# Products and sums of the modulation tables moved from VectorE to GpSimd, dealt out evenly from the third pair of feed-forward columns

## The chip, the cores and the metric

The kernel runs on one core of a Trainium2 chip. The metric is the device time of one execution in microseconds. Engines are named as in the profile: PE is TensorE, DVE VectorE, ACT ScalarE, POOL GpSimd, and SP the queue that issues the loads.

## The reference, cut to what matters

Two layers act on 256 rows of `x` and 256 rows of a context, 1024 wide. Each layer is a feed-forward, a mixer (gated linear attention, a short convolution, latent attention) and a second feed-forward. All are steered by modulation tables, nine parts of 1024 columns for each layer, made from one vector for `x` and one for the context:

```
for l in range(DEPTH):
    mod_x = jnp.split((sc @ ada_w[l] + ada_b[l])[:, None, :], N_MOD, axis=-1)
    mod_c = jnp.split((scc @ ada_w[l] + ada_b[l])[None, None, :], N_MOD, axis=-1)
    x = _ffn_step(x, mod_x, 0, ffn_w13[l, 0], ffn_w2[l, 0], ln_w[l, 0], ln_b[l, 0])
    ctx = _ffn_step(ctx, mod_c, 0, ffn_w13[l, 0], ffn_w2[l, 0], ln_w[l, 0], ln_b[l, 0])
    ...
```

`ada_w[l]` is 1024 x 9216 in fp32. `sc` and `scc` are single rows, so the two products read 38 MB a layer for two rows of output. In the last layer the context needs no parts 5 to 8.

## The kernel before, in words

**Weights.** Every large matrix is multiplied in three passes: a weight tile of 128 x 1024 fp32 is loaded by SP into one of five `raw` buffers (`NRAW`), ACT rounds it to `wh` (line 187), DVE takes the rest `wl = raw - wh` (line 188), and PE does wh by high, wh by low and wl by high (lines 232 to 235). There are three `wh` and three `wl` buffers (`NSPL`), and splits are made two tiles ahead (`AHEAD`). The order of all loads is that of the calls of `g.w`, recorded in a dry run of the program (`plan`); a load is issued as soon as one of the five buffers is free. Weight tiles and tiles of `ada_w` share this row and these buffers.

**Steps.** A feed-forward's first product (`ffn_in`) goes by 11 pairs of columns, p = 0 to 10, of 4 weight tiles each (two for `a`, two for `g`). One weight tile is one step: 24 matmuls with 512 columns. After a pair come SiLU, product and split (lines 730 to 735). Work left over from the stage before is called between steps: `pend` (transposes of the last rows) and `late` (renewing and storing the residual, lines 590 to 594).

**Modulation tables.** The first two parts of layer 0 are made on PE (`ada_group`). All others are made by the generator `ada_part` (lines 426 to 452): a part is eight tiles of `ada_w` of 128 x 1024; for each, DVE adds the tile times one column of `csil` to `acc`, for each stream (`x`, context) and each half of 512 columns. That is four DVE instructions a tile with two streams, two with one. Then PE sums `acc` over partitions with a matrix of ones (`pick`, line 448), DVE adds the bias to a `modrow` (line 384), and either POOL stores it to DRAM (line 387, parts 2, 5 and 8) or PE transposes it into `modT`. The bias tile `adab` is cleared by POOL (line 402) and loaded by SP (line 404).

A part has 12 units (`yield`) with two streams, 8 with one: one for each tile (two tiles with one stream), the rest for the end. `feeds` holds the parts under way. `feed(n)` runs n units; `feed_share(steps)` runs the units left over the steps left, rounded up. Units are dealt out at four places, which are called here by letters:

- **A**, the first feed-forward of layer 0: parts 2, 3, 4, two streams.
- **B**, the end of the mixer of layer 0: parts 5, 6, 7, two streams, one unit a step through `side`.
- **C**, the second feed-forward of layer 0: part 8, then parts 0 and 1 of layer 1, two streams.
- **D**, the first feed-forward of layer 1: parts 2, 3, 4 with two streams, 5 to 8 with one.

Each stage ends with `feed(10 ** 6)`: all its parts are done before the next begins.

**Buffers.** `T` is a pool of 9 tiles of 128 x 512, `U` one of 50. Before, `acc` lies in `T`, with `adab`, `modrow`, the `sil` tiles and the residuals `res`.

**POOL before** clears tiles, takes reciprocal roots for the norms (lines 581, 740 and 741) and issues some stores.

Of the kernel before, what the change touches and what calls it, by code (L numbers as in the profile page):

```python
# [13 lines left out]
ALU = mybir.AluOpType  # L14
# [8 lines left out]
NFB = DFF // P  # L23
# [275 lines left out]
def build(ctx, tc, aps, out, plan=None):  # L299

    g = Core(ctx, tc, aps, plan)
    nc = tc.nc
    act, dve, pe, pool, sp = nc.scalar, nc.vector, nc.tensor, nc.gpsimd, nc.sync
# [67 lines left out]
    csil = g.const([P, 8, 32], "csil")  # L371
# [8 lines left out]
    def ada_end(l, starts, ps, bias, streams):  # L380

        nq = 256
        row = g.T(name="modrow")
        dve.tensor_tensor(row[:, :nq], ps[:, :nq], bias[:, :nq], op=ALU.add)
        for q, c0 in enumerate(starts):
            if (c0 // D) % 3 == 2:
                pool.dma_start(modD[l][:streams, c0:c0 + nq], row[32 * q:32 * q + streams, :nq])
        yield
        if any((c0 // D) % 3 < 2 for c0 in starts):
            nj = nq // P  # L390
            pst = g.PS("adaT")
            for j in range(nj):
                transpose(pst[:, j * P:(j + 1) * P], row[:, j * P:(j + 1) * P])
            p4 = pst[:, :nj * P].rearrange("p (j q r) -> p q j r", j=nj, q=4)
            for q in (0, 2):
                k = starts[q] // P
                dve.tensor_copy(modT[l][:, k:k + 2 * nj, :].rearrange("p (q j) s -> p q j s", q=2), p4[:, q:q + 2, :, 0:2])
        yield

    def ada_bias(l, starts):  # L400
        bias = g.T(name="adab")
        pool.memset(bias[:, :256], 0.0)
        for q, c0 in enumerate(starts):
            sp.dma_start(bias[32 * q:32 * q + 2, :256], A_["ada_b"][l, c0:c0 + 256].partition_broadcast(2))
        return bias
# [20 lines left out]
    def ada_part(l, part, streams):  # L426


        starts = [part * D + 256 * q for q in range(4)]
        bias = ada_bias(l, starts)  # L430
        acc = [[g.T(name="acc") for _ in range(2)] for _ in range(streams)]
        for k in range(8):
            w = g.w([(R["ada_w"][l][k * P:(k + 1) * P, part * D:(part + 1) * D], D)], 1, split=False)
            for s_ in range(streams):
                for half in range(2):
                    a, b = acc[s_][half], w[:, 0, half * 512:(half + 1) * 512]
                    if k == 0:
                        dve.tensor_scalar(a, b, scalar1=csil[:, k, s_:s_ + 1], scalar2=None, op0=ALU.mult)
                    else:
                        dve.scalar_tensor_tensor(a, b, csil[:, k, s_:s_ + 1], a, op0=ALU.mult, op1=ALU.add)  # L440
            del w
            if streams == 2 or k % 2:
                yield
        yield
        ps = g.PS("ada")
        for s_ in range(streams):
            for q in range(4):
                pe.matmul(ps[32 * q:32 * q + 32, :256], pick[:, 1 - s_:33 - s_], acc[s_][q // 2][:, (q % 2) * 256:(q % 2 + 1) * 256],
                          start=s_ == 0, stop=s_ == streams - 1)
        del acc  # L450
        yield
        yield from ada_end(l, starts, ps, bias, streams)

    feeds = []

    def feed_parts(l, parts, streams=2):
        for part in parts:
            feeds.append([ada_part(l, part, streams), (8 if streams == 2 else 4) + 4])

    def feed(n):  # L460
        while n > 0 and feeds:
            try:
                next(feeds[0][0])
                feeds[0][1] -= 1
                n -= 1
            except StopIteration:
                feeds.pop(0)

    def feed_share(steps):

        left = sum(n for _, n in feeds)
        feed(-(-left // max(steps, 1)))

    def mod_ab(l, i, ln):

# [230 lines left out]
    def ffn_in(l, j, hT, tiles, gT, pend, late, opening=None):  # L706
        parts = parts_of(tiles)
        full = slice(0, parts[-1].stop)
        w13 = R["ffn_w13"][l, j]
        tiles_of = lambda c0, ps: g.fm_tiles(w13, c0, 8, g.pair_outs(ps), parts)  # L710
        psa, psg = {}, {}
        for p in range(NFB // 2):
            if p == 0 and opening is not None:
                psa[0], psg[0], psa[1] = [[g.PS("a") for _ in range(2)] for _ in range(3)]
                opening(tiles_of(0, psa[0]), tiles_of(DFF, psg[0]), tiles_of(256, psa[1]))
            else:
                tl = []
                if p not in psa:
                    psa[p] = [g.PS("a") for _ in range(2)]
                    tl += tiles_of(p * 256, psa[p])  # L720
                psg[p] = [g.PS("g") for _ in range(2)]
                tl += tiles_of(DFF + p * 256, psg[p])
                for n, _ in enumerate(g.fm(tl, hT, parts, group=3 if p == 0 and len(parts) > 1 else 1)):
                    if pend and n >= 1:
                        pend.pop(0)()
                    if late and p >= 1:
                        late.pop(0)()
                    feed_share(4 * (NFB // 2 - p) - 2 - n)
            for b in range(2):
                s = g.T(name="sil")  # L730
                act.activation(s[:, full], psa[p][b][:, full], AF.Silu)
                dve.tensor_tensor(s[:, full], s[:, full], psg[p][b][:, full], op=ALU.mult)  # L732
                h, lo = g.pairs(1, "g")[0]
                g.split(h[:, full], lo[:, full], s[:, full])
                gT.append((h, lo))
        feed(10 ** 6)
# [593 lines left out]
    for t in range(4):  # L1330
        a = A_["x"][0] if t < 2 else A_["ctx"][0]
# [23 lines left out]
    def opening(ta, tg, tb):  # L1355

        mm = lambda t, w, part, bs=(0, 1): g.mm3([(
            t[2][b][2][:, part], (w[0][:, kk, b * P:(b + 1) * P], w[1][:, kk, b * P:(b + 1) * P]),
            (hT[k][0][:, part], hT[k][1][:, part]), k == 0 and part.start == 0, k == 7 and part.stop == 512)
            for b in bs for kk, k in enumerate(t[1])], 0)  # L1360
        full = slice(0, 512)
        second = half_table(1)
        mod_ab0(0)
        bring((0, 1), 0)
        g.hold(2)
        wa, wg = g.w(ta[0][0], 4), g.w(tg[0][0], 4)
        for n, (t, w, part) in enumerate(((ta, wa, X), (tg, wg, X), (ta, wa, C), (tg, wg, C))):
            mm(t[0], w, part)
            if n == 0:
                bring((2, 3), 0)  # L1370
            if n == 1:
                g.early(1)
            next(second)
            next(second)
        del wa, wg, w
        next(second)
        g.early(1)
        wb = g.w(tb[0][0], 4)
        mm(tb[0], wb, full, (0,))
        run_all(second)  # L1380
        mod_ab0(1)
        bring((0, 1), 1)
        mm(tb[0], wb, full, (1,))
        g.hold(2)
        for t in (2, 3):
            load_x(t, 1)
        wa, wg = g.w(ta[1][0], 4), g.w(tg[1][0], 4)
        mm(ta[1], wa, X)
        bring((2, 3), 1)
        g.hold(None)  # L1390
        mm(tg[1], wg, X)
        mm(ta[1], wa, C)
        mm(tg[1], wg, C)
        wb = g.w(tb[1][0], 4)
        mm(tb[1], wb, full)
        feed_parts(0, (2, 3, 4))

    pend, late = [load_small] + [lambda: None] * 3 + [small_vectors], []
# [5 lines left out]
    for l in range(DEPTH):  # L1404
        last = l == DEPTH - 1
        tiles = [0, 1, 2, 3]
        if last:
            feed_parts(l, (2, 3, 4))
            feed_parts(l, (5, 6, 7, 8), 1)
        gT = []  # L1410
        ffn_in(l, 0, hT, tiles, gT, pend, late, opening if l == 0 else None)
        k1 = kept(f"h{l}a")
        pend, late = project_ln(gT, NFB, R["ffn_w2"][l, 0], tiles, l, 0, 0.5, ln_inputs(tiles, l, 0, res), k1, mod_ab(l, 1, (l, 0)),
# [10 lines left out]
        if not last:  # L1424
            feed_parts(l, (8,))
            feed_parts(l + 1, (0, 1))
        gT = []
        ffn_in(l, 1, hT, tiles, gT, pend, late)
        if last:
            o2 = out[0]  # L1430
# [15 lines left out]
def emit(tc, aps, out):  # L1446
    plan = build(None, Null(), {n: Null() for n in aps}, Null())
    with ExitStack() as ctx, tc.manual_schedule():
        build(ctx, tc, aps, out, plan)
# [18 lines left out]
```

## Time and profile before

| what | us |
|---|---|
| median of 3 runs (2699.78 to 2702.04) | 2700.31 |
| the profiled execution's own time | 2701.05 |
| its span in the profile | 2699.2 |
| PE busy in the span | 2621.2 |
| DVE busy | 1602.1 |
| ACT busy | 982.3 |
| POOL busy | 81.3 |

The sum of the prediction is made against the profiled execution, 2701.05 us; the median of the runs is 0.7 us lower. Busy times of the engines overlap. PE's mean granted clock over the span is 0.987 of full speed.

### The profile page before, as it was taken

What the parts mean: (1) busy time and instruction counts of PE and PEld (TensorE: products, weight loads), DVE (VectorE), ACT (ScalarE), POOL (GpSimd) and SP (SyncE); (2) the same over time, 40 slices, a digit from 0 to 9 for tenths busy, and PEclk for the clock granted to TensorE, in tenths of its full rate; (3) what the DMA queues carried; (4) which work ended last, traced back from release to release, by engine and by line L of the source; (5) the groups of instructions that cost most, each with busy time, mean ns of one, the idle gap of its engine ahead of it and who ended that gap; (6) DMA issues with size and microseconds to landing.
All of it is one profiled execution on the core that took longest, in us unless ns stands there. A gap on an engine that the chain in (4) does not pass through costs nothing. (4 is left out here: it accounts for less than half of the span.)

```text
span 2699.2 us, 36225 instructions
## 1 busy us (share of the span) xinstructions
PE 2621.2 (97%) x14243; PEld 2234.0 (83%) x14243; DVE 1602.1 (59%) x2429; ACT 982.3 (36%) x1565; POOL 81.3 (3%) x149
## 2 busy tenths in 40 slices
PE   8999999999999999999999979899999999999998
PEld 6888888888887888877888867788888988998996
DVE  3656256765453677468653389654367745567655
ACT  2222234545433232333222131223145653444442
POOL 0000000000000000000000000000010000100000
PEclk9999999999999999999999999899999999999999
DMA  7545353223221745546542456655443343567555
GB/s 251 175 152 164 114 166 98 67 63 120 78 75 59 226 150 155 165 134 194 169 137 98 157 159 206 213 175 168 154 133 102 108 130 100 174 179 227 180 188 171
DMA packets 324609, 400.63 MB, mean 148 GB/s; under 512 B 28403, under 2 KB 241935, under 8 KB 324439
## 3 DMA queue, kind: packets, MB, share of 16 engines
q1 hardware_dynamic: 321623, 391.99, 46.2%
q0 software_dynamic: 2816, 6.34, 0.6%
q8 instruction: 111, 1.82, 0.3%
q14 instruction: 59, 0.48, 0.1%
HBM read 382.49 MB, written 15.77 MB: 148 GB/s over the span
## 5 line engine op out<-in xcount | busy, mean ns | idle before, releaser
L188 DVE TENSOR_TENSOR wl<-raw,wh 128x1024 fp32r<-128x1024 f32 (+1 forms) x529 | 639.3, 1214 | 581.8 <-ACT wh L187 304.4
L187 ACT ACTIVATE wh<-raw 128x1024 fp32r<-128x1024 f32 (+1 forms) x529 | 549.0, 1050 | 794.2 <-PE tm L233 310.7
L232 PE MATMUL a<-hTh,wh 128*128 128x512 f32 (+1 forms) x784 | 271.0, 359 | 22.1 <-ACT wh L187 13.0
L440 DVE SCALAR_TENSOR_TENSOR acc<-raw,csil,acc 128x512 f32<-128x512 f32 x392 | 267.7, 749 | 0.0
L233 PE MATMUL a<-hTl,wh 128*128 128x512 f32 (+1 forms) x752 | 260.7, 359 | 1.3 <-DVE hTl L531 1.0
L232 PE MATMUL g<-hTh,wh 128*128 128x512 f32 (+1 forms) x704 | 247.3, 362 | 3.9 <-ACT wh L187 3.9
L233 PE MATMUL g<-hTl,wh 128*128 128x512 f32 (+1 forms) x688 | 241.2, 361 | 0.0
L232 PE MATMUL tm<-wh,gh 128*128 128x512 f32 x616 | 240.3, 390 | 0.0
L233 PE MATMUL tm<-wh,gl 128*128 128x512 f32 x616 | 239.7, 389 | 0.0
L232 PEld LDWEIGHTS a<-hTh,wh 128*128 128x128 f32 x784 | 153.2, 195 | 48.8 <-ACT wh L187 14.2
L233 PEld LDWEIGHTS a<-hTl,wh 128*128 128x128 f32 x752 | 146.9, 195 | 21.7 <-DVE hTl L531 2.6
L235 PE MATMUL tm<-wl,gh 128*128 128x512 f32 x616 | 163.4, 390 | 0.6 <-DVE wl L188 0.6
L235 PE MATMUL a<-hTh,wl 128*128 128x512 f32 (+1 forms) x752 | 157.9, 352 | 0.8 <-DVE wl L188 0.8
L232 PEld LDWEIGHTS g<-hTh,wh 128*128 128x128 f32 x704 | 134.0, 190 | 26.6 <-ACT wh L187 4.5
L240 ACT ACTIVATE gh<-sil 128x512 fp32r<-128x512 f32 (+1 forms) x88 | 50.9, 578 | 279.3 <-DVE sil L732 279.3
L235 PE MATMUL g<-hTh,wl 128*128 128x512 f32 (+1 forms) x688 | 149.4, 359 | 0.0
L233 PEld LDWEIGHTS g<-hTl,wh 128*128 128x128 f32 x688 | 130.6, 190 | 19.2
L235 PEld LDWEIGHTS a<-hTh,wl 128*128 128x128 f32 x752 | 125.9, 191 | 19.8 <-DVE wl L188 1.0
L235 PEld LDWEIGHTS tm<-wl,gh 128*128 128x128 f32 x616 | 115.4, 188 | 25.7 <-DVE wl L188 1.9
L233 PEld LDWEIGHTS tm<-wh,gl 128*128 128x128 f32 x616 | 115.7, 188 | 23.8
L232 PEld LDWEIGHTS tm<-wh,gh 128*128 128x128 f32 x616 | 115.6, 188 | 23.8
L235 PEld LDWEIGHTS g<-hTh,wl 128*128 128x128 f32 x688 | 117.9, 189 | 19.4
(323 smaller groups left out, 4705.0 us busy)
## 6 DMA issues: line engine op xcount, KB each, us to landing
raw<-in_ffn_w_dram SPq DMA_DIRECT2D x279, 512.0 KB
raw<-in_w_in_dram SPq DMA_DIRECT2D x156, 512.0 KB
raw<-in_ada_w_dram SPq DMA_DIRECT2D x128, 512.0 KB
raw<-in_w_out_dram SPq DMA_DIRECT2D x20, 512.0 KB
raw<-in_ada_w_dram SPq DMA_DIRECT2D x32, 256.0 KB
raw<-in_mla_proj_dram SPq DMA_DIRECT2D x16, 512.0 KB
raw<-in_gla_proj_dram SPq DMA_DIRECT2D x16, 512.0 KB
raw<-in_conv_proj_dram SPq DMA_DIRECT2D x16, 512.0 KB
```

The lines of the kernel that those rows point to most:

```text
L187: nc.scalar.activation(hi[:, :n], raw[:, :n], AF.Copy)
L188: nc.vector.tensor_tensor(lo[:, :n], raw[:, :n], hi[:, :n].bitcast(F32), op=ALU.subtract)
L232: mm(out, lhs[0], rhs[0], start=start, stop=False)
L233: mm(out, lhs[late], rhs[1 - late], start=False, stop=False)
L235: mm(out, lhs[1 - late], rhs[late], start=False, stop=stop)
L240: nc.scalar.activation(hi, src, AF.Copy)
L440: dve.scalar_tensor_tensor(a, b, csil[:, k, s_:s_ + 1], a, op0=ALU.mult, op1=ALU.add)
```

## The change

DVE's `acc = raw * csil + acc` becomes two POOL instructions, a product into a new `T` tile `prod` and a sum; a part's first tile needs the product alone. `acc` moves from `T` to `U`. `feed_share` keeps a running fraction in place of rounding up, it is called from p = 2 on and only where no `late` job is called, and it aims at an end within the last pair. The unit counts come out as before (12 and 8).

```diff
-        acc = [[g.T(name="acc") for _ in range(2)] for _ in range(streams)]
+        acc = [[g.U(name="acc") for _ in range(2)] for _ in range(streams)]
...
-                    if k == 0:
-                        dve.tensor_scalar(a, b, scalar1=csil[:, k, s_:s_ + 1], scalar2=None, op0=ALU.mult)
-                    else:
-                        dve.scalar_tensor_tensor(a, b, csil[:, k, s_:s_ + 1], a, op0=ALU.mult, op1=ALU.add)
+                    to = a if k == 0 else g.T(name="prod")
+                    pool.tensor_scalar(to, b, scalar1=csil[:, k, s_:s_ + 1], scalar2=None, op0=ALU.mult)
+                    if k:
+                        pool.tensor_tensor(a, a, to, op=ALU.add)
...
-            feeds.append([ada_part(l, part, streams), (8 if streams == 2 else 4) + 4])
+            feeds.append([ada_part(l, part, streams), 8 * streams // 2 + 4])
...
+    owed = [0.0]
+
     def feed_share(steps):
 
-        left = sum(n for _, n in feeds)
-        feed(-(-left // max(steps, 1)))
+        owed[0] += sum(n for _, n in feeds) / max(steps, 1)
+        n = int(owed[0])
+        owed[0] -= n
+        feed(n)
...
                     if late and p >= 1:
                         late.pop(0)()
-                    feed_share(4 * (NFB // 2 - p) - 2 - n)
+                    elif p >= 2:
+                        feed_share(4 * (NFB // 2 - 1 - p) + 2 - n)
```

How the instructions stand, at three places.

SP in stage D, before: the loads behind the first weight tiles (`in_ffn_w_dram`) of the stage; `in_ada_w_dram` are tiles of the modulation tables.

```order
L176 DMA raw_12304<-in_ffn_w_dram 128x4x256
L176 DMA raw_12352<-in_ffn_w_dram 128x4x256
L176 DMA raw_12360<-in_ffn_w_dram 128x4x256
L176 DMA raw_12380<-in_ada_w_dram 128x1024
L176 DMA raw_12432<-in_ada_w_dram 128x1024
L176 DMA raw_12464<-in_ada_w_dram 128x1024
L176 DMA raw_12512<-in_ada_w_dram 128x1024
L176 DMA raw_12526<-in_ada_w_dram 128x1024
L404 DMA adab_12552<-in_ada_b_dram 2x256 x4
L176 DMA raw_12566<-in_ada_w_dram 128x1024
```

With the change, SP in stage D from the 12th weight tile on (`h0c` is the stored residual, a `late` job):

```order
L176 DMA raw_13288<-in_ffn_w_dram 128x4x256
L598 DMA h0c<-r_12568 128x512
L176 DMA raw_13321<-in_ffn_w_dram 128x4x256
L598 DMA h0c<-r_12822 128x512
L176 DMA raw_13354<-in_ada_w_dram 128x1024
L598 DMA h0c<-r_12603 128x512
L176 DMA raw_13387<-in_ada_w_dram 128x1024
L598 DMA h0c<-r_12843 128x512
L176 DMA raw_13438<-in_ffn_w_dram 128x4x256
L598 DMA h0c<-r_12650 128x512
L176 DMA raw_13471<-in_ada_w_dram 128x1024
L176 DMA raw_13504<-in_ada_w_dram 128x1024
```

The eight tiles that stood behind the third weight tile now begin behind the 13th, two to a weight tile.

DVE in stage D, before, a weight tile's split with the sums around it:

```order
L188 TENSOR_TENSOR wl_13142<-raw_13002,wh_13141 128x1024
L438 TENSOR_SCALAR acc_13137<-raw_12990,csil 128x512
L438 TENSOR_SCALAR acc_13138<-raw_12990,csil 128x512
L438 TENSOR_SCALAR acc_13139<-raw_12990,csil 128x512
L438 TENSOR_SCALAR acc_13140<-raw_12990,csil 128x512
L440 SCALAR_TENSOR_TENSOR acc_13137<-raw_12996,csil,acc_13137 128x512
L440 SCALAR_TENSOR_TENSOR acc_13138<-raw_12996,csil,acc_13138 128x512
L440 SCALAR_TENSOR_TENSOR acc_13139<-raw_12996,csil,acc_13139 128x512
L440 SCALAR_TENSOR_TENSOR acc_13140<-raw_12996,csil,acc_13140 128x512
```

With the change, DVE in stage D where the first part is under way:

```order
L188 TENSOR_TENSOR wl_13613<-raw_13438,wh_13612 128x1024
L188 TENSOR_TENSOR wl_13663<-raw_13616,wh_13662 128x1024
L188 TENSOR_TENSOR wl_13721<-raw_13666,wh_13720 128x1024
L188 TENSOR_TENSOR wl_13779<-raw_13724,wh_13778 128x1024
L188 TENSOR_TENSOR wl_13799<-raw_13738,wh_13798 128x1024
```

DVE's queue holds the splits and a pair's end alone.

POOL in stage D, before: the whole of its work for parts 2 to 4.

```order
L402 MEMSET adab_12552 128x256
L387 DMA modD_100<-modrow_12791 2x256 x4
L402 MEMSET adab_12823 128x256
L402 MEMSET adab_13131 128x256
L402 MEMSET adab_13409 128x256
```

With the change, POOL from the end of part 2 (its last tile, 13694) to the second tile of part 3:

```order
L438 TENSOR_SCALAR prod_13810<-raw_13694,csil 128x512
L440 TENSOR_TENSOR acc_13610<-acc_13610,prod_13810 128x512
L438 TENSOR_SCALAR prod_13813<-raw_13694,csil 128x512
L440 TENSOR_TENSOR acc_13611<-acc_13611,prod_13813 128x512
L387 DMA modD_100<-modrow_13869 2x256 x4
L402 MEMSET adab_13905 128x256
L438 TENSOR_SCALAR acc_13911<-raw_13752,csil 128x512
L438 TENSOR_SCALAR acc_13912<-raw_13752,csil 128x512
L438 TENSOR_SCALAR acc_13913<-raw_13752,csil 128x512
L438 TENSOR_SCALAR acc_13914<-raw_13752,csil 128x512
L438 TENSOR_SCALAR prod_13945<-raw_13796,csil 128x512
L440 TENSOR_TENSOR acc_13911<-acc_13911,prod_13945 128x512
```

The store of a gate part's `modrow` (line 387) stands in POOL's queue between the sums of that part and the products of the next.

## Rows read from the trace of the kernel before

**Rows 1.** The page: the span, and PE's line (busy us, share, count).

```profile
span 2699.2 us, 36225 instructions
PE 2621.2 (97%) x14243; PEld 2234.0 (83%) x14243; DVE 1602.1 (59%) x2429; ACT 982.3 (36%) x1565; POOL 81.3 (3%) x149
```

**Rows 2.** Busy time by stretch: stages A, B, C, a second product (22 tiles), D.

```profile
core 0: us, PE busy (x) PEld busy (x) DVE busy (x) ACT busy (x) POOL busy (x), PEclk, DMA share, GB/s
59.00:292.00 233.00, 233.00 (x1086) 191.72 (x1085) 142.65 (x197) 68.24 (x89) 2.88 (x6) 1.00 0.48 156
...
877.00:1167.00 290.00, 289.66 (x1311) 237.06 (x1310) 179.87 (x241) 82.29 (x99) 7.13 (x14) 1.00 0.56 173
...
1216.00:1473.00 257.00, 251.66 (x1178) 207.33 (x1178) 158.89 (x220) 76.76 (x103) 2.74 (x6) 0.99 0.48 152
1473.00:1595.00 122.00, 121.48 (x585) 101.94 (x583) 59.82 (x81) 36.42 (x54) 4.40 (x5) 1.00 0.46 147
1595.00:1885.00 290.00, 261.89 (x1196) 210.44 (x1197) 199.03 (x287) 73.40 (x94) 8.34 (x18) 0.95 0.58 191
```

**Rows 3.** PE's waits in stage D (us in total, times, longest).

```profile
PE ada L448 <- DVE acc L440: 12.0, 1, 12.0
PE a L232 <- ACT wh L187: 9.0, 2, 5.0
```

**Rows 4.** SP's waits over the span, the largest.

```profile
SPq L176 <- DVE wl L188: 1583.2, 446, 12.5
SPq L176 <- DVE acc L440: 213.8, 109, 6.5
```

**Rows 5.** POOL's wide and small instructions, ns min/median/max: lines 1164, 402, 740.

```profile
L1164 POOL MEMSET Tm<- x12: 516/522/528, 688.7 to 2197.2; 128x512 f32 x12
...
L402 POOL MEMSET adab<- x18: 311/313/479, 1.2 to 1773.8; 128x256 f32 x18
...
L740 POOL TENSOR_SCALAR oss<-oss x6: 192/193/193, 828.2 to 2307.7; 128x4 f32<-128x4 f32 x6
```

**Rows 6.** POOL in order of time, two dependent instructions (start us, us).

```profile
432.93 0.19 POOL L740 TENSOR_SCALAR ss<-ss 128x1 f32<-128x1 f32 x1 [24.61 <-ACT sq L765]
433.20 0.55 POOL L741 TENSOR_TENSOR ss<-ss,mhalf 128x1 f32<-128x1 f32 x1
```

**Rows 7.** POOL and DVE in order of time at 390 us.

```profile
389.99 1.57 POOL L581 TENSOR_TENSOR rs<-rs,mhalf 128x1 f32<-128x1 f32 x1 [2.15 <-DVE rs L580]
...
389.84 1.23 DVE L188 TENSOR_TENSOR wl<-raw,wh 128x1024 fp32r<-128x1024 f32 x1
```

**Rows 8.** DVE's groups in stage D (busy us, mean ns of one).

```profile
L440 DVE SCALAR_TENSOR_TENSOR acc<-raw,csil,acc 128x512 f32<-128x512 f32 x138 | 94.2, 747 | 0.0
L188 DVE TENSOR_TENSOR wl<-raw,wh 128x1024 fp32r<-128x1024 f32 x46 | 56.3, 1223 | 34.0 <-ACT wh L187 19.9 <-PE g L235 4.4 <-PE a L235 4.2
L241 DVE TENSOR_TENSOR gl<-sil,gh 128x512 fp32r<-128x512 f32 x22 | 15.2, 693 | 15.3 <-ACT gh L240 15.3
...
L438 DVE TENSOR_SCALAR acc<-raw,csil 128x512 f32<-128x512 f32 x16 | 7.0, 491 | 0.0
```

**Rows 9.** DVE's groups with two SBUF inputs in stage B, 945 to 1167 us.

```profile
L1037 DVE SCALAR_TENSOR_TENSOR z<-cu,sv,z 128x510 f32<-128x510 f32 x8 | 6.0, 751 | 6.8 <-ACT z L1035 6.8
L1038 DVE SCALAR_TENSOR_TENSOR z<-cu,sv,z 128x510 f32<-128x510 f32 x8 | 6.0, 750 | 0.3
L241 DVE TENSOR_TENSOR cvl<-z,cvh 128x512 fp32r<-128x512 f32 x8 | 5.5, 693 | 5.6 <-ACT cvh L240 5.6
```

## The prediction

> **What bounds the kernel now.** I read the page first: PE is busy 2621.2 of 2699.2 us, DVE 1602.1, POOL 81.3 [rows 1]. So the kernel is PE's, and relieving DVE can only give back time in which PE waits. I then asked for busy time by stretch, one for each stage in which modulation parts are made [rows 2]. In A and B PE has nothing to give: it is busy 233.00 of 233 us and 289.66 of 290. In C it lacks 5.3 us, and its granted clock is 0.99, which over 257 us is worth 2.6 more: about 8 us. In D it lacks 28.1 us, and the clock of 0.95 over 290 us is worth 14.5: 42.6 us. PE's waits in D name the reason: one of 12.0 us for DVE's sums, others for weight splits that come late [rows 3], while DVE is busy 199 of 290 us there, 101.2 of it with the sums [rows 2, 8]. All that the change can win is thus about 43 + 8 = 51 us.
>
> A step (one weight tile) costs PE 122 / 22 = 5.5 us, from the second product with no parts in it [rows 2]. Loads wait mostly for DVE's splits to free a buffer [rows 4]: the ring of five `raw` buffers is always full, so whoever holds one longer delays the weights.
>
> **The POOL instructions.** Before shows no wide POOL instruction that reads. What it shows: clearing 128x512 takes 522 ns and 128x256 takes 313, so 0.82 ns a column, 0.42 us for one pass of 512; a small scalar product takes 0.19 us [rows 5]. The nearest price of a product is 0.19 + 0.42 = **0.61 us**; if reading and writing were separate passes it would be 1.03. An add has two inputs: 0.19 + 2 x 0.42 = 1.03 us if they come one behind the other, 1.45 with a third pass for the write. DVE does two reads and a write of 1024 columns in 1.22 us [rows 8], 1.19 ns a column, so a write beside the reads is usual here; I take **1.15 us**, nearer the low end. The add waits for its own product; between two dependent POOL instructions lie 433.20 - (432.93 + 0.19) = 0.08 us [rows 6]. A tile with two streams costs POOL 4 x (0.61 + 1.15 + 0.08) = 7.4 us, the first tile of a part 2.4, a part 54.0 us, a part with one stream 27.0.
>
> The Trainium skill (GPSIMD Engine Reference, section 3.1) speaks against this change: it gives 4497 ns for an add of 2048 columns on GpSimd, 1.96 times VectorE's time, and no run here shows it yet. In proportion that is an estimate of 1.12 us for 512 columns, and by it the sum below would come to about 2828.
>
> **What POOL shares with DVE.** A one-column power takes POOL 0.55 us [rows 6], but 1.57 when it starts 0.15 us into a split of DVE's [rows 7]: it waited for the split's remaining 1.08 us. Hence I let POOL lose the time of every DVE instruction with two SBUF inputs: a step has one split of 1.22 us and, a pair of `gl` in four steps, 2 x 0.69 / 4 = 0.35 [rows 8], 1.57 us in all. In B, six steps hold four convolution terms of 0.75 and two `cvl` of 0.69 [rows 9], so a step there takes 1.95. At the other end the loss is zero, if wide instructions share.
>
> **Stage by stage.** POOL need not follow PE's position: a tile can be worked on when its load has landed, and it must be done before its buffer is wanted. With five buffers and three splits I count a window of five steps, 27.5 us, for a tile that itself costs 7.4 + 1.57; 18.6 us can be lagged before PE waits.
>
> - **D.** 68 units fall on 32 steps. 160 products and 140 adds make 3 x 54.0 + 4 x 27.0 = 270 us. The first part's tile is 13 weight tiles into the stage and loads five entries ahead, so POOL starts some six steps and a landing, 36 us, in. Behind its last add come two steps, the pair's end and `pick`, 13 us. To end in 290 us POOL would have 241. Splits cost 36 x 1.57 = 57 us. The store of parts 2 and 5 stands in POOL's queue ahead of the next products and waits for PE and `modrow`: between nothing and two steps, I take one each, 11 us. 270 + 57 + 11 = 338, **+97 us**; DVE's old stalls are in this, since the stage is then paced by POOL.
> - **A.** 36 units on 36 steps, a tile a step. A part costs 54.0 + 8 x 1.57 = 66.6 us against eight steps of PE, 44; the lag of 22.6 exceeds 18.6 by 4, three times: **+12**. The gap of four units behind each part lets POOL catch up.
> - **B.** Part 5 lies among steps without units and is hidden. Parts 6 and 7 run a tile a step: 54.0 + 15.6 - 44 - 18.6 = 7, **+14**.
> - **C.** `late` now takes the steps of p = 1 and 2, so 36 units fall on 32 steps and eight tiles on seven: 54.0 + 11 - 38.5 - 18.6 = 7.9, three times 24. The tiles that crowded the stage's start are gone, which gives back its 8 us: **+16**.
>
> Edits that I cost at nothing: `acc` in `U` (44 tiles of `g` pairs and 4 of `acc` stay under 50), the `adab` clears (0.31 us), and `pick`, which stays on PE. `prod` takes turns in `T` with `sil`; were that cover gone, POOL could start later than assumed, which is in the upper end. Stores on line 1011 stand behind sums in B; their readers come a branch later. DVE's relief is worth nothing once POOL sets the pace.
>
> Sum: 97 + 12 + 14 + 16 = 139; 2701.05 + 139 = **2840 us**, as much over the profiled execution, itself 0.7 us above the median.
>
> Bounds: with adds of 1.03 and no wait for the stores a part is 50.6 us, and the stages give 69 + 2 + 7 + 5 = 83: 2785. With adds of 1.45 and two steps for each store a part is 62.4, and they give 150 + 37 + 31 + 41 = 259: 2960.
>
> **Rivals.**
>
> - *POOL keeps pace, faster.* Then the late splits of D and the crowded start of C go: 2701 - 43 - 8 = 2650. In its favour: 12.0 us in one wait for the sums [rows 3]. Against it: even with nothing lost to DVE, POOL fits into D's 241 us only if an add takes (241 - 98) / 140 - 0.08 = 0.94 us, and gives the whole gain only at 0.64, below two passes. Chance 0.07. Just at 0.94 to 1.03 the two cancel (2705 at 1.03): no change, 0.03.
> - *No loss beside DVE.* POOL is as slow as I say but a wide read does not wait for a split. Then only D remains, 270 + 11 - 241 = 40, less 8: 2733, down to 2705 with fast adds. For it: the power that waited is a small instruction of another kind. Against it: 1.57 to 0.55. Chance 0.15.
> - *Separate passes.* A product of 1.03 and an add of 1.45 make a part 75.8 us: 217 + 77 + 58 + 81 = 433, up to 3134. Against it: DVE's 1.19 ns a column. Chance of more than 2975: 0.10.
>
> **How the numbers follow.** My forecast, POOL as the pace of D and partly of A to C, has 0.65 and its own range 2785 to 2960. The range 2705 to 2975 adds the second rival and the neighbourhood of the upper bound, and leaves out the fast and the very slow case. A measurement of this kernel tells about 0.2%, 5.4 us, from no change: faster 0.07, same 0.03, slower 0.90.
>
> **What would show it.** Products near 0.61 us and adds near 1.15, longer where a split runs; POOL busy some 800 us; PE's waits in D on POOL's `acc` and on late weight loads, with SP waiting for POOL; D some 390 us long, A to C 10 to 25 longer; the granted clock of D lower than 0.95. I am wrong if POOL idles in D, if PE waits there for something other than sums or loads behind them, or if A to C grow more than D.

## The result and the profile after

The changed kernel takes 3259.98 us in the median of four runs (3255.99 to 3261.32), the kernel before 2700.26 in the same measurement: a ratio of 1.2071, 95% interval 1.2052 to 1.2090. The forecast was 2840 us, with a range up to 2975: the direction and the four stages were right, the size was a quarter of what came, and stages A to C, foreseen at 42 us together, took more than half of it.

The page of the changed kernel, beside [rows 1]: busy us, share, count, and the costliest POOL groups (their mean ns behind the busy time).

```profile
span 3259.2 us, 36604 instructions
PE 2745.9 (84%) x14243; PEld 2292.7 (70%) x14243; DVE 1392.5 (43%) x1981; ACT 987.0 (30%) x1565; POOL 1382.0 (42%) x989
...
L438 POOL TENSOR_SCALAR prod<-raw,csil 128x512 f32<-128x512 f32 x392 | 695.2, 1773 | 15.3 <-DMA raw<-in_ada_w_dram 11.3
L440 POOL TENSOR_TENSOR acc<-acc,prod 128x512 f32<-128x512 f32 x392 | 522.9, 1334 | 32.7
```

The same 14243 matmuls now fill 84% of the span. The product, for which the prediction had 0.61 us, has a mean of 1.77; the sum, foreseen at 1.15, has 1.33.

Busy time by stretch of the changed kernel, beside [rows 2]: A, B with some work ahead of it, C and D.

```profile
core 0: us, PE busy (x) PEld busy (x) DVE busy (x) ACT busy (x) POOL busy (x), PEclk, DMA share, GB/s
49.00:388.00 339.00, 259.92 (x1108) 204.54 (x1107) 103.12 (x107) 70.99 (x95) 286.79 (x187) 0.86 0.35 111
975.00:1357.00 382.00, 319.27 (x1300) 251.29 (x1301) 135.89 (x147) 84.62 (x107) 284.74 (x191) 0.90 0.41 129
1405.00:1775.00 370.00, 277.83 (x1199) 220.27 (x1200) 119.67 (x136) 75.01 (x102) 283.51 (x189) 0.85 0.33 105
1896.00:2434.00 538.00, 300.42 (x1236) 229.82 (x1235) 127.06 (x138) 75.13 (x102) 465.09 (x321) 0.75 0.32 104
```

The same stage D in the kernel before, from PE's first to its last matmul there ([rows 2] begins 11 us later):

```profile
1584.00:1873.60 289.60, 261.17 (x1234) 211.41 (x1233) 204.49 (x297) 73.92 (x102) 10.61 (x21) 0.95 0.59 193
```

In D POOL is now busy 465 of 538 us and PE 300; before, PE was busy 261 of 290. DVE falls from 204 us to 127 there, and nothing comes of it. DMA moves 104 GB/s there, 193 before, so bandwidth is no bound.

Where PE waits, and what the loads wait for, over the span (us in total, times, longest), beside [rows 3, 4]:

```profile
PE ada L448 <- POOL acc L440: 245.8, 50, 26.7
PE a L232 <- ACT wh L187: 89.0, 12, 19.9
PE g L232 <- ACT wh L187: 88.4, 11, 19.2
...
SPq L176 <- DVE wl L188: 1464.1, 360, 13.1
SPq L176 <- POOL prod L438: 983.7, 106, 13.5
```

Two paths lead from POOL to PE, as foreseen. One is direct: PE sums `acc` over partitions and POOL's last sum is not there. The other is by buffers: SP waits 984 us for POOL's products to free a `raw` tile, so weights land late, ACT rounds them late, and PE waits for `wh`. In D alone:

```profile
PE ada L448 <- POOL acc L440: 159.0, 20, 26.7
PE a L232 <- ACT wh L187: 52.7, 7, 19.9
PE g L232 <- ACT wh L187: 25.8, 2, 19.2
```

The first path costs PE 159 us there and the second 79, together the 238 us in which it is not busy.

The 560 us lie in the four stages alone. Their lengths, from PE's matmuls in the profile of each kernel (A from the end of the two parts that PE makes itself, B from the end of the gated linear attention's outputs to the first product with `w_out`), with the runs told of below:

| kernel | A | B | C | D | median us |
|---|---|---|---|---|---|
| before | 232.9 | 297.9 | 257.4 | 289.6 | 2700.3 |
| the change | 339.4 | 391.3 | 369.0 | 537.6 | 3260.0 |
| dealing alone (e1) | 233.1 | 297.9 | 252.2 | 304.8 | 2711.1 |
| GpSimd alone, old dealing (e2) | 322.0 | 393.8 | 381.3 | 512.1 | 3232.8 |
| VectorE's product (e3) | 267.5 | 326.8 | 290.5 | 395.3 | 2903.3 |
| ScalarE's product (e4) | 242.9 | 301.9 | 271.0 | 344.6 | 2787.1 |
| product as tensor by tensor (e5) | 303.6 | 358.9 | 332.3 | 462.3 | 3080.6 |
| product with a constant (e6) | 327.6 | 382.6 | 358.8 | 514.5 | 3207.2 |
| product in two halves (e7) | 364.4 | 420.0 | 401.0 | 578.9 | 3389.5 |
| sums alone (e8) | 248.1 | 317.0 | 273.8 | 332.2 | 2791.8 |
| sums alone with a break (e9) | 245.5 | 304.9 | 262.2 | 340.0 | 2776.3 |
| even from the second pair, VectorE (v1) | 233.5 | 297.9 | 251.1 | 283.5 | 2691.3 |
| v1, a quarter of D's tiles on GpSimd (v2) | 234.0 | 297.9 | 251.1 | 302.1 | 2706.8 |
| v1 with six raw buffers (v4) | 233.0 | 297.9 | 252.8 | 277.6 | 2683.8 |

The change adds 106.5 + 93.4 + 111.6 + 248.0 = 559.5 us. How POOL spends D, in order of time in the changed kernel (start us, us):

```profile
1937.36 6.81 POOL L438 TENSOR_SCALAR acc<-raw,csil 128x512 f32<-128x512 f32 x4 [29.88 <-DMA raw<-in_ada_w_dram]
...
2001.44 1.26 POOL L440 TENSOR_TENSOR acc<-acc,prod 128x512 f32<-128x512 f32 x1
2002.68 1.56 POOL L438 TENSOR_SCALAR prod<-raw,csil 128x512 f32<-128x512 f32 x1
2004.33 1.26 POOL L440 TENSOR_TENSOR acc<-acc,prod 128x512 f32<-128x512 f32 x1
...
2412.99 1.26 POOL L440 TENSOR_TENSOR acc<-acc,prod 128x512 f32<-128x512 f32 x1
2416.20 2.00 POOL L387 DMA_DIRECT2D modD<-modrow  x4 [1.94 <-DVE modrow L384]
```

It begins 41 us into the stage and goes on from 1937 to 2414 us with under 5 us of waits in between, a product and its sum every 2.89 us where VectorE does not lengthen them (2001.44 to 2004.33). It stops 20 us before the stage ends at 2434.

### The profile page after: what moved, and what is told of

Its sections match the earlier page's. It is cut to its first block, busy times and chain, and to the rows that moved or that the text cites. A ratio compares the mean times of both kernels' runs of the same rounds, so it can differ in the third digit from the quotient of the medians.

```text
span 3259.2 us, 36604 instructions
## 1 busy us (share of the span) xinstructions
PE 2745.9 (84%) x14243; PEld 2292.7 (70%) x14243; DVE 1392.5 (43%) x1981; ACT 987.0 (30%) x1565; POOL 1382.0 (42%) x989
## 5 line engine op out<-in xcount | busy, mean ns | idle before, releaser
L188 DVE TENSOR_TENSOR wl<-raw,wh 128x1024 fp32r<-128x1024 f32 (+1 forms) x529 | 677.7, 1289 | 1090.9 <-ACT wh L187 823.6
L438 POOL TENSOR_SCALAR prod<-raw,csil 128x512 f32<-128x512 f32 x392 | 695.2, 1773 | 15.3 <-DMA raw<-in_ada_w_dram 11.3
L440 POOL TENSOR_TENSOR acc<-acc,prod 128x512 f32<-128x512 f32 x392 | 522.9, 1334 | 32.7
L585 POOL TENSOR_TENSOR rs<-rs,mhalf 128x1 f32<-128x1 f32 x20 | 21.0, 1052 | 900.4 <-DVE rs L584 900.4
L232 PE MATMUL a<-hTh,wh 128*128 128x512 f32 (+1 forms) x784 | 289.6, 383 | 95.1 <-ACT wh L187 89.0
L232 PE MATMUL g<-hTh,wh 128*128 128x512 f32 (+1 forms) x704 | 267.0, 390 | 88.4 <-ACT wh L187 88.4
L233 PE MATMUL a<-hTl,wh 128*128 128x512 f32 (+1 forms) x752 | 276.7, 380 | 1.6 <-DVE hTl L535 1.5
L448 PE MATMUL ada<-acc,pick 128*32 128x256 f32 x224 | 54.8, 599 | 245.8 <-POOL acc L440 245.8
L233 PE MATMUL g<-hTl,wh 128*128 128x512 f32 (+1 forms) x688 | 257.4, 385 | 0.0
L448 PEld LDWEIGHTS ada<-acc,pick 128*32 128x32 f32 x224 | 10.0, 136 | 283.5 <-POOL acc L440 282.9
L232 PE MATMUL z<-hTh,wh 128*128 128x512 f32 (+1 forms) x384 | 131.7, 362 | 24.9 <-ACT wh L187 24.8
```

Source lines behind the costliest of these rows:

```text
L188: nc.vector.tensor_tensor(lo[:, :n], raw[:, :n], hi[:, :n].bitcast(F32), op=ALU.subtract)
L232: mm(out, lhs[0], rhs[0], start=start, stop=False)
L233: mm(out, lhs[late], rhs[1 - late], start=False, stop=False)
L438: pool.tensor_scalar(to, b, scalar1=csil[:, k, s_:s_ + 1], scalar2=None, op0=ALU.mult)
L440: pool.tensor_tensor(a, a, to, op=ALU.add)
L585: pool.tensor_tensor(rs, rs, mhalf[:, 0:1], op=ALU.pow)
```

## The experiments

The theory after the result: GpSimd's own pace sets the stages, by the prediction's own working, and only the price of an instruction was wrong. Rivals: the new dealing does it; GpSimd's instructions are long because VectorE runs beside them; or buffers are held by a second engine, at whatever price.

### Which half of the change: e1 and e2

e1 keeps the dealing and `acc` in `U` and gives the work back to VectorE:

```diff
-                    to = a if k == 0 else g.T(name="prod")
-                    pool.tensor_scalar(to, b, scalar1=csil[:, k, s_:s_ + 1], scalar2=None, op0=ALU.mult)
-                    if k:
-                        pool.tensor_tensor(a, a, to, op=ALU.add)
+                    if k == 0:
+                        dve.tensor_scalar(a, b, scalar1=csil[:, k, s_:s_ + 1], scalar2=None, op0=ALU.mult)
+                    else:
+                        dve.scalar_tensor_tensor(a, b, csil[:, k, s_:s_ + 1], a, op0=ALU.mult, op1=ALU.add)
```

> The changed dealing and acc in U, but products and sums on VectorE in one instruction as before. Theory (GpSimd's own pace sets the length of stages A to D): nearly all of the 560 us goes; the start of C gives back some 8 us, D stays within 20 us of its 290 because VectorE then has 24 tiles of four sums (3.0 us each) in some 16 steps of 5.5 us beside 1.6 us of splits; 2680 to 2710. Rival (the later and even dealing itself, with acc in U, holds the weights up): at least 50 us over before, 2750 or more.

Measured: 2711.1 us, ratio 1.0043 (1.0030 to 1.0056). That is 1 us over the theory's upper end and far under the rival's 2750: the engine costs 549 us, the dealing 11. C gives back 5.2 us, as its start is no longer crowded; D loses 15.2.

e2 is the reverse, the kernel before with products and sums on GpSimd and `acc` in `U`; its old dealing begins with a stage's first pair.

> Products and sums on GpSimd with acc in U, but the old dealing (rounded up, from the second pair on). Theory: GpSimd's work is the same, it only starts earlier in A, C and D, by some 5 to 10 steps of 5.5 us in each: 3110 to 3240. Rival (dealing is the cause): under 2800.

Measured: 3232.8 us, ratio 1.1975 (1.1959 to 1.1991). The engine alone costs 533 us. Beside the change, GpSimd starts earlier in A, C and D. A and D are 17 and 25 us shorter; C is 12 us longer, where I had expected it shorter too, and why is open.

### What the product costs: e5, e6 and e7

e5 runs the product through the two-tensor form:

```diff
-                    pool.tensor_scalar(to, b, scalar1=csil[:, k, s_:s_ + 1], scalar2=None, op0=ALU.mult)
+                    pool.tensor_tensor(to, b, csil[:, k, s_:s_ + 1].to_broadcast([P, 512]), op=ALU.mult)
```

> As the change, but the product as a GpSimd tensor-by-tensor product with the column of csil spread over 512 columns (step 0), so that GpSimd never runs its scalar form. Theory: if the scalar form is what is slow, a product costs what the sum costs, 1.28 us; the working then gives D +217, A +84, B +62, C +88: about 3150. Rival (any product of that tile costs 1.57 us): 3260 within 20.

e6 takes a constant (`scalar1=0.5`) in place of the column.

> As the change, but the product takes the constant 0.5 in place of csil's column, so the modulation tables of all parts but the first two of layer 0 are left out of the computation. Theory A (the pointer to the column makes the scalar form slow): 0.6 to 0.8 us a product and some 2880. Theory B (the form itself is slow on GpSimd at this width): 1.57 us and 3260 within 20.

e7 makes each product in two instructions:

```diff
-                    pool.tensor_scalar(to, b, scalar1=csil[:, k, s_:s_ + 1], scalar2=None, op0=ALU.mult)
+                    for c in range(2):
+                        cc = slice(256 * c, 256 * c + 256)
+                        pool.tensor_scalar(to[:, cc], b[:, cc], scalar1=csil[:, k, s_:s_ + 1], scalar2=None, op0=ALU.mult)
```

> As the change, each product in two instructions of 256 columns. Tells the fixed part of the scalar form from its price a column. Theory (a price a column, over a fixed 0.19 us as the 128x4 form takes): 0.88 us for 256 columns, 0.19 us more a product, some 85 us more in all, about 3340. Rival (a large fixed part, the columns at a clear's 0.82 ns): 1.35 us for 256 columns and 3700 or more.

The product's row in the change, then in e5, e6 and e7, from the view of its line (ns minimum/median/maximum, first and last start):

```profile
L438 POOL TENSOR_SCALAR prod<-raw,csil x392: 1553/1566/3597, 68.0 to 2411.3; 128x512 f32<-128x512 f32 x196
```

```profile
L438 POOL TENSOR_TENSOR prod<-raw,csil x392: 1029/1040/2036, 70.7 to 2231.2; 128x512 f32<-128x512 f32 x196
```

```profile
L438 POOL TENSOR_SCALAR prod<-raw x392: 1478/1490/2494, 69.3 to 2357.9; 128x512 f32<-128x512 f32 x196
```

```profile
L440 POOL TENSOR_SCALAR prod<-raw,csil x784: 912/922/2953, 67.5 to 2539.4; 128x256 f32<-128x256 f32 x196
```

And the sum's in the change:

```profile
L440 POOL TENSOR_TENSOR acc<-acc,prod x392: 1259/1283/2356, 69.7 to 2413.0; 128x512 f32<-128x512 f32 x196
```

The minima lie beside the medians, so a product costs 1.56 us with nobody in its way; VectorE adds only the difference to the mean. It is the scalar form as such: a constant saves 5% (1.49), and the two-tensor form, whose second operand is one column repeated, needs 1.04. e5's total, 3080.6 us (ratio 1.1411, 1.1393 to 1.1428), lies below what I expected, because I gave it the sum's 1.28. From 922 ns for 256 columns and 1566 for 512, the scalar form costs 2.52 ns a column over a fixed 0.28 us; the prediction had 0.82 and 0.19. e7 comes to 3389.5 us in its one run, near the 3340 of a price by the column and far from 3700: it pays the fixed part 448 times more, 125 us of the 130 that it takes over the change. e6's 3207.2, in its one run, fits the second theory in kind; it is 53 us under the change, where 20 at most were expected, and its products sum to 50 us less.

### Products on another engine: e3 and e4

e3 makes the product with `dve.tensor_scalar`, e4 with ScalarE; the sum stays on GpSimd.

```diff
-                    pool.tensor_scalar(to, b, scalar1=csil[:, k, s_:s_ + 1], scalar2=None, op0=ALU.mult)
+                    act.activation(to, b, AF.Copy, scale=csil[:, k, s_:s_ + 1])
```

> As the change, but the product on VectorE (0.48 us in the trace of before), only the sum on GpSimd. Theory with the working of the prediction and the measured sum of 1.28 us: GpSimd has 140 x 1.36 = 190 us in D beside 57 us lost to splits, against 241: +17; nothing in A and B, 8 us back in C: about 2710, 2690 to 2740. Rival (any wide GpSimd instruction in the chain from raw to acc holds loads up, whatever its price): 2850 or more.

> As the change, but the product on ScalarE (Copy with a column of csil as scale), the sum on GpSimd. It differs from the run with VectorE's product in the engine of the product alone. Theory (there, VectorE's one-input product waited for GpSimd's sum beside it, 1.5 us in place of 0.48, and the two serialised): ScalarE's product keeps about 0.6 us beside a sum of 1.28, D has 190 + 57 + 11 us of GpSimd work against 241, and the whole takes 2700 to 2760. Rival (sums on GpSimd hold loads up whoever makes the product): within 40 of 2903.

The product's row in e3, and in e4:

```profile
L438 DVE TENSOR_SCALAR prod<-raw,csil x392: 469/1499/1525, 87.5 to 2051.8; 128x512 f32<-128x512 f32 x196
...
L438 DVE TENSOR_SCALAR acc<-raw,csil x56: 477/481/616, 84.8 to 2027.3; 128x512 f32<-128x512 f32 x56
```

```profile
L438 ACT ACTIVATE prod<-raw,csil x392: 703/709/727, 87.8 to 1931.5; 128x512 f32<-128x512 f32 x196
```

e3 took 2903.3 us (ratio 1.0754, 1.0740 to 1.0769): by its total the rival was right, and the theory's upper end is missed by 163 us. But the row gives another reason. A part's first products, the `acc` row, take VectorE 0.48 us; of the later ones most take 1.50, though they have one input. The 1.0 us is waiting for a sum on GpSimd: of the 259 later products that begin while a sum runs, 257 take 1.4 us or more, and of the 133 others none takes over 0.8. So the two engines take turns. In e4, with the same sums, ScalarE's products stay at 0.71 us in all 392 cases and the kernel takes 2787.1 (1.0322, 1.0308 to 1.0336). That is 116 us less than e3, as the theory wanted in direction, and 27 more than its upper end. D is 55 us longer than before. PE waits 43 us there for GpSimd's sums, and GpSimd 106 us for ScalarE's products, 64 of them before its first sum: ScalarE's queue holds the products between the weights' rounding. VectorE's splits meet the sums too, one of them for 12.9 us:

```profile
1733.05 12.91 DVE L188 TENSOR_TENSOR wl<-raw,wh 128x1024 fp32r<-128x1024 f32 x1 [4.71 <-ACT wh L187]
```

How much each makes of the 55 us was not tried.

### GpSimd's sums with no one else: e8 and e9

e8 leaves the products out, but for each part's first tile:

```diff
-                    to = a if k == 0 else g.T(name="prod")
-                    pool.tensor_scalar(to, b, scalar1=csil[:, k, s_:s_ + 1], scalar2=None, op0=ALU.mult)
-                    if k:
-                        pool.tensor_tensor(a, a, to, op=ALU.add)
+                    if k == 0:
+                        pool.tensor_scalar(a, b, scalar1=csil[:, k, s_:s_ + 1], scalar2=None, op0=ALU.mult)
+                    else:
+                        pool.tensor_tensor(a, a, b, op=ALU.add)
```

> As the change, but the products of all but a part's first tile are left out (the tile itself is added), so the modulation tables are not those of the reference. GpSimd then does 392 sums and 56 products and no other engine takes part. Theory (the stages last as long as GpSimd's instructions): a part costs 28 x 1.32 + 4 x 1.57 = 43 us, which A, B and C cover, and D has 216 + 44 lost to VectorE and stores against 231: 2715 to 2745. Rival (loads held by a second engine, whatever it costs): 2800 or more.

Measured: 2791.8 us (1.0333, 1.0312 to 1.0354), 47 us over the theory's upper end and 8 under the rival's 2800. D, +43 us, came as worked out (216 + 44 - 231 = 29) within 14, but A, B and C are 15 to 19 us longer each, where nothing was expected. Part of the reason shows in the order of time around 1378 us in e8, POOL and then DVE:

```profile
1373.68 27.03 POOL L440 TENSOR_TENSOR acc<-acc,raw 128x512 f32<-128x512 f32 x22
...
1376.51 0.69 DVE L737 TENSOR_TENSOR sil<-sil,g 128x512 f32<-128x512 f32 x1 [8.27 <-PE g L235]
1377.95 23.31 DVE L241 TENSOR_TENSOR gl<-sil,gh 128x512 fp32r<-128x512 f32 x1 [0.76 <-ACT gh L240]
1401.18 0.68 DVE L737 TENSOR_TENSOR sil<-sil,g 128x512 f32<-128x512 f32 x1
```

A 0.69 us instruction of VectorE with two SBUF inputs waited 23 us, until a row of 22 sums of GpSimd, with no gap between them, was over; 18 of these began after it. Six others took 6.7 to 23.8 us in the same profile, each up to the end of such a row. But that is not the rule: of the 97 splits and `gl` that begin during a sum in e8, 92 are done within 2.4 us, 62 of them with three or more sums of the row still to come. What decides is open. In the change each sum waits for its product, and nothing on VectorE takes over 2.4 us; in e5, where product and sum both have the two-tensor form, nothing takes over 3 us. e9 tests whether breaks in the rows are enough, with one small waiting instruction after each tile's sums:

```diff
+            pool.tensor_scalar(a[:, :1], a[:, :1], scalar1=1.0, scalar2=None, op0=ALU.mult)
             del w
```

> As the run with sums alone (products left out, so the modulation tables are not those of the reference), and after each tile's four sums one GpSimd instruction of one column that waits for the last of them. Theory (in the run with sums alone VectorE's two-input instructions, up to 23.8 us long, waited for an unbroken row of GpSimd sums; any break lets them in): none over 6.5 us, A, B and C within 8 us of the kernel before, D at 320 to 345 since GpSimd has some 12 us more to do there; 2725 to 2760 in all. Rival (the row of sums is not what held VectorE): 2792 within 12, with waits over 10 us still there.

The splits' rows in e8 and in e9:

```profile
L188 DVE TENSOR_TENSOR wl<-raw,wh x529: 946/1225/23849, 18.7 to 2775.2; 128x1024 fp32r<-128x1024 f32 x170, 128x768 fp32r<-128x768 f32 x7
```

```profile
L188 DVE TENSOR_TENSOR wl<-raw,wh x529: 947/1225/2396, 18.6 to 2754.4; 128x1024 fp32r<-128x1024 f32 x170, 128x768 fp32r<-128x768 f32 x7
```

The long waits are gone: nothing on VectorE takes over 2.4 us. B and C come within 7 and 5 us of before. A stays 12.6 over, so its one long wait was not what lengthened it, and the cause there is open. D is at 340, inside its span; of GpSimd's 128 extra instructions (mean 0.50 us, where 0.2 was foreseen) 56 fall into it. The total, 2776.3 us (1.0287, 1.0270 to 1.0305), misses the expected upper end by 16 us, which was set too low: the stages at their expected ends already make 2779.

### A version that beats both: v1, v2 and v4

If the crowded starts of C and D were all that could be won, the running fraction should do it on VectorE, dealt from the second pair beside the `late` jobs (v1, from the kernel before):

```diff
-        left = sum(n for _, n in feeds)
-        feed(-(-left // max(steps, 1)))
+        owed[0] += sum(n for _, n in feeds) / max(steps, 1)
+        n = int(owed[0])
+        owed[0] -= n
+        feed(n)
...
-                    feed_share(4 * (NFB // 2 - p) - 2 - n)
+                    if p >= 1:
+                        feed_share(4 * (NFB // 2 - p) - 2 - n)
```

> The kernel before with only the running fraction, dealt from the second pair on beside the late jobs, VectorE doing products and sums. Theory (D and the start of C lost time only because units were crowded at the first pair): C gives back 5 us as with the dealing alone, D drops from 290 to 265 to 280; 2675 to 2690. Rival (VectorE is the bound of D's middle however units are dealt): D stays within 8 us of 290, 2690 to 2700.

Measured: 2691.3 us, ratio 0.9969 (0.9956 to 0.9981). C is 6.3 us shorter, D 6.1: faster than before, but by the rival's measure. v2 hands one of four half-tiles in D's two-stream parts to GpSimd:

```diff
+                    if l == 1 and part > 1 and s_ == 1 and half == 1:
+                        to = a if k == 0 else g.T(name="prod")
+                        pool.tensor_tensor(to, b, csil[:, k, s_:s_ + 1].to_broadcast([P, 512]), op=ALU.mult)
+                        if k:
+                            pool.tensor_tensor(a, a, to, op=ALU.add)
-                    if k == 0:
+                    elif k == 0:
```

> As the kernel with the fraction from the second pair, and in D GpSimd takes one of four halves of each two-stream tile (context, second half of the columns) as two tensor-by-tensor instructions of 1.04 and 1.28 us. Theory: 24 tiles x 2.4 = 58 us fit beside some 20 steps of 5.5, VectorE's load in that stretch drops by 18 us, D takes 255 to 270; 2665 to 2685, at or under the kernel without GpSimd. Rival (what GpSimd does beside VectorE's splits delays these more than it relieves): slower than that kernel by 5 us or more.

It took 2706.8 us (1.0028, 1.0018 to 1.0037): 15 us slower than v1, and D alone is 18.6 longer. VectorE's remaining sums have two SBUF inputs, and in this profile they reach 1784 ns against 752 in v1's. In D, v2 and then v1:

```profile
L445 DVE SCALAR_TENSOR_TENSOR acc<-raw,csil,acc 128x512 f32<-128x512 f32 x119 | 97.9, 883 | 0.0
L440 DVE SCALAR_TENSOR_TENSOR acc<-raw,csil,acc 128x512 f32<-128x512 f32 x140 | 95.3, 745 | 0.0
```

The 119 sums that are left take VectorE more time than the 140 did. So even 62 us of GpSimd's work costs more than it relieves, in this form at least: `prod` also takes a place in `T` beside `acc` here, and what that costs was not tried.

v4 is v1 with a sixth `raw` buffer (`NRAW` 6; `acc` in `U`, 49 tiles there and 8 in `T`, to make room).

> The kernel with the fraction from the second pair on VectorE, with six raw buffers in place of five (acc in U, 49 and 8 tiles in U and T). Theory (what is left of D's loss is loads that come late behind bunches of table tiles, since ScalarE waited 175 us for weights there): D falls from 283 to 272 to 280; 2680 to 2688. Rival (VectorE's own pace holds D): 2691 within 3.

Measured: 2683.8 us, ratio 0.9941 (0.9927 to 0.9955): the fastest of all, 0.6% under the kernel before. D is 277.6 us, within the expected span (the 175 us that the expectation names are ScalarE's wait over all of v1; in D it is 107). D in v4 by the view of busy time:

```profile
1580.00:1858.00 278.00, 260.69 (x1236) 211.07 (x1235) 204.28 (x299) 73.51 (x102) 10.02 (x21) 0.97 0.62 201
```

PE still lacks 17 us there, at a clock of 0.97. Whether the sixth buffer or the places of `acc` bring the 7 us over v1 was not told apart.

## Why the prediction was wrong

**The bound and the ceiling.** Right. DVE's relief won nothing: by [rows 2] PE could gain back some 50 us at most, and the runs that dealt better on VectorE (v1, v4) got 8 and 16 of them.

**The price of the product.** This is the step that failed. The prediction took a product as a fixed 0.19 us and one pass at the rate of POOL's clears, 0.61 us [rows 5]; a product of 1.03 stood in its third rival alone. It costs 1.57. A clear only writes, and the small scalar products behind the 0.19 us read one to four columns: neither shows what reading a column costs in the scalar form. I treated that form as the cheaper, since it reads one tensor; e5 shows the two-tensor form 0.53 us faster. The range was no bound on this: both of its ends kept the product at 0.61 and moved the sum, the stores and the loss to VectorE alone, though that price came from a row of another operation.

**The price of the sum.** 1.15 against 1.28, 10% low, and inside its ends. That it came so near is luck: the same reckoning by passes gave 0.61 for the product. The estimate of 1.12 us in proportion to the figure of the Trainium skill (GPSIMD Engine Reference, section 3.1) came out low by 12%.

**The working.** With the measured 1.566 and 1.283 us, a part costs 7 x 4 x 2.849 + 4 x 1.566 = 86.0 us and the lag that a tile allows shrinks to 27.5 - 11.4 - 1.57 = 14.5. The same sums as on record then give, beside what was measured:

| stage | on record | with measured prices | measured |
|---|---|---|---|
| A | 12 | 3 x (86.0 + 12.6 - 44 - 14.5) = 120 | 106.5 |
| B | 14 | 2 x (86.0 + 15.6 - 44 - 14.5) = 86 | 93.4 |
| C | 16 | 3 x (86.0 + 11 - 38.5 - 14.5) - 8 = 124 | 111.6 |
| D | 97 | 430 + 57 + 11 - 241 = 257 | 248.0 |
| sum | 139 | 587 | 559.5 |

The stages were sized from the right mechanism: put into the sums on record, the product's price alone gives 567 us in place of 139, the sum's alone 191. The working magnifies it: by the numbers on record a part in A is hidden up to 44 + 18.6 - 12.6 = 50 us, and beyond that every us counts.

**The smaller terms of D.** POOL began 41 us into the stage (36 on record) and ended 20 us before its end (13). The wait of the stores was smaller than one step each: POOL's waits there sum to 5.8 us. What POOL lost to VectorE is 33 us, where 57 stood: the products and sums of D take 243.1 + 32.7 + 182.2 = 458 us, and 160 and 140 of the shortest (1.553 and 1.259 us) would take 425.

**Not every meeting costs.** The prediction let every two-input instruction of VectorE take its time from POOL [rows 7]. A split beside the POOL rows shown above, and a second meeting, POOL and then VectorE:

```profile
2003.21 1.24 DVE L188 TENSOR_TENSOR wl<-raw,wh 128x1024 fp32r<-128x1024 f32 x1 [9.10 <-ACT wh L187]
...
2015.87 1.26 POOL L440 TENSOR_TENSOR acc<-acc,prod 128x512 f32<-128x512 f32 x1
2017.11 2.00 POOL L438 TENSOR_SCALAR prod<-raw,csil 128x512 f32<-128x512 f32 x1
...
2016.29 1.39 DVE L241 TENSOR_TENSOR gl<-sil,gh 128x512 fp32r<-128x512 f32 x1 [0.69 <-ACT gh L240]
```

The split at 2003.21 begins half a us into a product and both keep their lengths; the `gl` at 2016.29 begins in a sum and doubles, and the product behind that sum takes 2.00 us. Over the whole profile of the change, 74 of the 108 splits and `gl` that begin during a product keep their length, and 65 of the 73 that begin during a sum are longer. So the cost falls on either engine, depending on how they meet. The second rival, no loss at all, is nonetheless refuted by the 33 us above and by the mean product of 1.77 us against a shortest of 1.55.

**The signs.** POOL is busy 1382 us where 800 stood, and PE waits in D for the two things named. But one sign of being wrong came: A to C grew more than D, by 311 us together against 248, though each by less. The working with the measured prices gives that too (330 and 257): a part in A to C was on record just past what its lag hides, so nearly the whole error in the price shows there, once for each of eight parts.

**The chances.** Slower had 0.90 and came; the range of the forecast itself, with 0.65, missed. The very slow rival (0.10, separate passes for reading and writing) was nearest, and its 3134 us is still 126 short.

## What to carry to other kernels

Price each form of a GpSimd instruction by a run of that form: neither a clear nor a small instance, nor the number of inputs, tells what a wide one costs. An engine that paces a stage through shared buffers is invisible until its work for a part outgrows the lag that the buffers allow, and then every further microsecond shows, so a term near that edge needs the widest bounds. Before work is moved to an idle engine, ask how much the bound engine can win back: here it was 51 us, under 2% of the span, and an even dealing on the old engine, with a sixth buffer and `acc` in `U`, took 0.6% without GpSimd.

## What the runs showed that I had not expected

- GpSimd's scalar product of 512 fp32 columns takes 1.57 us, with a constant 1.49; the same product as tensor by tensor, the second operand one column repeated, takes 1.04. A sum of two full tensors takes 1.28.
- An unbroken row of GpSimd sums can hold a two-input VectorE instruction until the row ends: 23.3 us for 0.69, and six more cases in e8. Most are let in sooner (92 of 97 within 2.4 us), and what decides is open. With one instruction that waits for the last sum, after every fourth, none takes over 2.4 us (e9). The Trainium skill (SBUF — State Buffer, "SBUF: two separate sides") says that whichever of the two starts first gets the pair of memory ports that they share for the whole instruction. The trace shows that the wait can go on over 18 more instructions.
- VectorE's one-input product of fp32 tiles waits for GpSimd too: 1.50 us in place of 0.48 (e3).
- PE's mean granted clock in D, over stretches at 2.4 and at 1.2 GHz, fell to 0.75, from 0.95 before, while its waits there grew from 28 us to 238; as many recorded matmuls (1236 and 1234) were busy 300 us in place of 261.
